# Conditioning vectors summed along rows on VectorE in place of TensorE products

## The chip, the cores and the metric

The kernel runs on one core of a Trainium2 chip. The metric is device time in microseconds (us). The engines of the core work side by side, each on its own queue: TensorE (PE for its matmuls, PEld for its weight loads), VectorE (DVE), ScalarE (ACT), GpSimd (POOL) and SyncE (SP), which here issues the loads from HBM.

## The reference

The program is one layer of a decoder trunk on 256 tokens of 2048 channels, all in fp32. A vector c of 2048 values conditions it: six vectors of 2048 channels (shift, scale and gate of two sub-layers) come from one product with a matrix of 2048 x 12288.

```python
c_act = jax.nn.silu(c)
mod = (c_act @ w_ada[l] + b_ada[l])[:, None, :]
sh1, sc1, g1, sh2, sc2, g2 = jnp.split(mod, 6, axis=-1)
h = layer_norm(x) * (1.0 + sc1) + sh1
y = token_mixer(h, w_in[l], ...)
x = layer_norm(ALPHA * x + g1 * y, ln_g[l, 0], ln_b[l, 0])
h = layer_norm(x) * (1.0 + sc2) + sh2
y = conv_ffn(h, w_up[l], ...)
x = layer_norm(ALPHA * x + g2 * y, ln_g[l, 1], ln_b[l, 1])
```

The token mixer is an input projection (`h @ w_in`), a sparse attention, a matrix memory, merge gates, branch projections and an output projection. `conv_ffn` is a gated MLP with 5632 hidden channels.

## The kernel before

All weights come in tiles of 128 x 1024 fp32 (512 KB) into six buffers `w`, by one queue on SP, in the order of use (`load`, L85). A weight of a projection is split into a high part `wh` (ACT, L96) and a low part `wl` (DVE, L97), with four buffers each, and a product is three fp32r matmuls, high x high, high x low and low x high (`mm_a`, `mm_b`, `mm_c`; all are recorded at L77). The order on each engine is set when the program is built: the code gives an order, and a scheduler moves instructions by its own model of time. On the chip each engine takes its list strictly in order.

**Conditioning.** `w_ada` (192 tiles) passes through the same six buffers. A tile holds 128 input channels (on partitions) by 1024 output channels. For one unit of 1024 outputs, DVE takes 16 tiles in turn and adds tile times c into `acc` (128 x 1024): the first with a `tensor_scalar` (L155), the other 15 with a `scalar_tensor_tensor` whose scalar is a column of c (L157), each reading the `acc` that the last one wrote. Then TensorE sums `acc` over the partitions by a product with ones. For shift and scale (`ada_cols`) the first unit does this with 16 small matmuls that put channels on partitions (tile `ps_ada`); the other seven units make a row (`ps_ada`, 32 x 512), ACT copies it out (L181) and two small DMAs issued by ACT turn it into columns `raw`. For the gates (`ada_rows`, four units) the product is 128 x 512 (`ps_adar`), so that the row stands on every partition, and DVE adds the bias, which is loaded broadcast (`badar`).

**Order of the work.** x (2 MB) is loaded, its mean and variance are taken (L249), it is normalised (L279) and turned channel-first by TensorE (`ps_nT`, `nT`). The input projection goes in four groups of four row chunks (512 channels). A group needs the shift and scale of its own 512 channels (one unit of 16 tiles): ACT scales the chunk (`hm`, L299), writes the high part of `hT` (L301) and DVE the low part (L302). Then come 288 matmuls `ps_b` and 144 matmuls `ps_a`, and the partial sums go to `accC`, `KT`, `accQ`, `accM` and `projA` (ACT in the first group, DVE adds L501 and L532 later). While a group runs, a ticker (`Ticker`, `tk`) hands out the 16 tiles of the next group's unit, one for each weight tile. Units of the second shift and scale, and of the gate g1, go out in the same way from the fourth group to the output projection (`ps_o`), and g2 goes out in the first half of the MLP's up projection (`ps_up`). Between `ps_o` and `ps_up` the residual is normalised twice (L890, L895, L922, L947, L949), with the normalised tile `n2` written in an order of channels that fits the columns of shift and scale: channel 512 q + 4 p + i on partition p. The weights' rows are packed in that order on the host.

Of the kernel before, what the change touches and what calls it, by code (L numbers as in the profile page):

```python
# [14 lines left out]
P = 128  # L15
# [17 lines left out]
GR = (1.0, 1.0)  # L33
# [5 lines left out]
FIRST = 14  # L39
F0 = 1  # L40
PTV = 2
YA, YB = 1, 2
# [9 lines left out]
def build(ctx: ExitStack, tc: tile.TileContext, d, out, dbg=None):  # L52
# [15 lines left out]
    nc.sync.dma_start(cst, d["cst"])  # L68
    ident = cst[:, C_ID:C_ID + P]
# [75 lines left out]
    # ---------------------------------------------------------------- conditioning  # L145
# [4 lines left out]
    def ada_partial(u):  # L150
        acc = p0.tile([P, 1024], F32, name="acc", tag="acc")
        for k in range(KD):
            t = load(d["w_ada"][u * KD + k])
            if k == 0:
                nc.vector.tensor_scalar(acc, t, cs[:, 0:1], None, op0=ALU.mult)  # L155
            else:
                nc.vector.scalar_tensor_tensor(acc, t, cs[:, k:k + 1], acc, op0=ALU.mult, op1=ALU.add)  # L157
            if k < KD - 1:
                yield
        yield acc  # L160

    def ada_cols(u, m_sh, m_sc, q):
        """Shift and 1 + scale of the channels 512 q + 4 p + i, on partition p, in column 4 q + i."""
        for acc in ada_partial(u):
            if acc is None:
                yield
        for _ in range(YA):
            yield
        ps = bank(psa, "ps_ada")
        if q == 0 and m_sh == 0:  # L170
            src = [ps[:, 4 * i:4 * i + 4] for i in range(2)]
            for i in range(2):
                v = acc[:, i * 512:(i + 1) * 512].rearrange("k (c b) -> k b c", b=4)
                for b in range(4):
                    mm(src[i][:, b:b + 1], v[:, b, :], ones[:, 0:1], True, True)
        else:
            raw = p0.tile([P, 2, 4], F32, name="raw", tag="raw", bufs=2)
            for i in range(2):
                mm(ps[32 * i:32 * i + 32, :], ones[:, 0:32], acc[:, i * 512:(i + 1) * 512], True, True)
            row = t2([64, 512], "row")  # L180
            nc.scalar.copy(row, ps[0:64, :])  # L181
            for i in range(2):
                nc.scalar.dma_start(raw[:, i, :], row[32 * i:32 * i + 1, :])
            src = [raw[:, i, :] for i in range(2)]
            for _ in range(YB):
                yield
        for i, m in ((0, m_sh), (1, m_sc)):
            c0 = m * KD + 4 * q
            nc.vector.tensor_add(modc[:, m, 4 * q:4 * q + 4], src[i],
                                 prm[:, R_BADA + c0:R_BADA + c0 + 4])  # L190
        nc.vector.tensor_scalar(modc[:, m_sc, 4 * q:4 * q + 4], modc[:, m_sc, 4 * q:4 * q + 4],
                                1.0, None, op0=ALU.add)
        yield

    def ada_rows(u, dst, col, c):
        """1024 gate values on every partition."""
        for acc in ada_partial(u):
            if acc is None:
                yield
        for i in range(2):  # L200
            c0 = c * 1024 + i * 512
            bt = t2([P, 512], "badar")
            nc.sync.dma_start(bt, d["b_ada"][0:1, col + c0:col + c0 + 512].to_broadcast([P, 512]))
            ps = bank(psa, "ps_adar")
            mm(ps, ones, acc[:, i * 512:(i + 1) * 512], True, True)
            nc.vector.tensor_add(dst[:, c0:c0 + 512], ps, bt)
# [30 lines left out]
    # ---------------------------------------------------------------- input norm  # L237
# [4 lines left out]
    xt = p0.tile([P, 2, D], F32, name="xt", tag="t16")  # L242
    for t in range(2):
        for c in (0, 1024):
            nc.sync.dma_start(xt[:, t, c:c + 1024], d["x"][t * P:(t + 1) * P, c:c + 1024])
# [22 lines left out]
    first = ada_cols(0, 0, 1, 0)  # L268
    for _ in range(FIRST):
        next(first)  # L270
# [10 lines left out]
    def turn(p):  # L281
        ps = bank(psa, "ps_nT")
        for i in range(2):
            for t in range(2):
                q, b = divmod(2 * p + i, 4)
                v = xt[:, t, q * 512:(q + 1) * 512].rearrange("s (c b) -> s b c", b=4)
                nc.tensor.transpose(ps[:, (2 * i + t) * P:(2 * i + t + 1) * P], v[:, b, :], ident)
# [5 lines left out]
    run_all(first)  # L293

    def modulate(dst, src_of, m_sh, m_sc, p):
        tmp = t2([P, 2, S], "hm")
        for i in range(2):
            k = 2 * p + i
            nc.scalar.activation(tmp[:, i, :], src_of(i), AF.Identity, bias=modc[:, m_sh, k:k + 1],  # L299
                                 scale=modc[:, m_sc, k:k + 1])  # L300
        nc.scalar.copy(dst[:, 2 * p:2 * p + 2, 0, :], tmp)  # L301
        nc.vector.tensor_sub(dst[:, 2 * p:2 * p + 2, 1, :], tmp, dst[:, 2 * p:2 * p + 2, 0, :])  # L302

    # ---------------------------------------------------------------- input projection
# [81 lines left out]
    tb = 0  # L386
    def modulate_in(p):
        modulate(hT, lambda i: nT[:, 2 * p + i, :], 0, 1, p)

    def ada_mod(q):  # L390
        yield from ada_cols(q, 0, 1, q)
        for p in (2 * q, 2 * q + 1):
            modulate_in(p)
            yield

    for p in range(2):
        modulate_in(p)
# [4 lines left out]
    # ---------------------------------------------------------------- gates  # L402
# [66 lines left out]
    for gi in range(4):  # L469
        nxt = gi < 3  # L470
        if nxt:
            tk.add(ada_mod(gi + 1))
        comp = []

        def work():
# [3 lines left out]
            tk.tick(GR[0] if nxt else GR[1])  # L479

        kn = 4
        k0 = 4 * gi
        for b0 in range(0, NBLK, 2):
            wh, wl = load_split(d["w_in_b"][tb])
            tb += 1
            work()
            for bb in range(2):
                b = b0 + bb
                if b % 2 == 0:
                    ps = bank(psm, "ps_b")  # L490
                for k in range(kn):
                    mm_b(ps[:, (b % 2) * S:(b % 2 + 1) * S], wh, wl, bb * kn + k, hT, k0 + k,
                         k == 0, k == kn - 1)
                if b % 2 == 1:
                    dst, kind = dest_b(b // 2)
                    src = (ps.rearrange("p (w t k) -> p w t k", w=2, t=2) if kind
                           else ps.rearrange("p (a b) -> p a b", a=2))
                    if gi == 0:
                        nc.scalar.copy(dst, src)
                    else:  # L500
                        nc.vector.tensor_add(dst, src, dst)  # L501
                    if not nxt and b == 3:
                        comp.append(compress())
                        for q in range(4):
                            tk.add(ada_cols(6 + q, 3, 4, q))
                    if not nxt and b == NBLK - 1:
                        conv()
        for c in range(6):
            pss = [bank(psm, "ps_a%d" % t) for t in range(2)]
            aw = AW if c < 4 else 512  # L510
            for pi in range(2):
                if c < 4:
                    wh, wl = load_split(d["w_in_a"][gi * 8 + c * 2 + pi])
                else:
                    wh, wl = load_split(d["w_in_v"][gi * 4 + (c - 4) * 2 + pi])
                work()
                for i in range(2):
                    k = k0 + 2 * pi + i
                    for t in range(2):
                        mm_a(pss[t][:, :aw], hT, k, t, wh[:, i * aw:(i + 1) * aw],  # L520
                             wl[:, i * aw:(i + 1) * aw], k == k0, k == k0 + kn - 1)
                if not nxt and c > 2:
# [10 lines left out]
            if not nxt:  # L533
                if c == 2:
# [4 lines left out]
                    next(steps)  # L539
        if nxt:  # L540
# [665 lines left out]
```

## Time and profile before

| | us |
|---|---|
| median of 3 runs (lowest, highest) | 1520.63 (1519.89, 1527.04) |
| span of the profiled execution | 1516.5 |
| median less span (start and end around the span) | 4.1 |
| TensorE matmuls busy | 1457.4 (96%) |
| VectorE busy | 1112.6 (73%) |
| ScalarE busy | 727.0 (48%) |
| moved by DMA | 376.98 MB, 249 GB/s in the mean |

The profile is of one execution. Its span runs from the first to the last instruction; its own device time was not recorded apart, so the median stands for it. A busy TensorE is not TensorE at its peak, since matmuls overlap: the chain of work that ended last shows the rate at which they follow each other.

### The profile page before, as it was taken

Reading aid. Unit: us, or ns where it says so; the run is one execution under the profiler, and the core shown is the slowest. Engines: PE = TensorE matmul, PEld = TensorE weight load, DVE = VectorE, ACT = ScalarE, POOL = GpSimd, SP = SyncE. Lnnn points to the kernel's source line nnn. Section 1 sums busy time; section 2 is a strip of 40 time slices with the busy share of each in tenths; the row PEclk is TensorE's granted clock in tenths of the full one; section 3 lists DMA queues with packets and bytes.
Section 4 is the critical chain, followed back from the end, with each engine's and each line's share of the span. In section 5 each row is a group of like instructions: output and inputs, shape, how many; then the busy total and the mean of one; then the engine's idle time right before and its main releaser. Section 6 shows DMA issues by size and latency. Waiting matters only on the chain.

```text
span 1516.5 us, 23668 instructions
## 1 busy us (share of the span) xinstructions
PE 1457.4 (96%) x9174; PEld 1299.5 (86%) x9174; DVE 1112.6 (73%) x1478; ACT 727.0 (48%) x1031; POOL 2.1 (0%) x6
## 2 busy tenths in 40 slices
PE   1999999999999999999699999999999999999997
PEld 1999898888889999988688888888898888888887
DVE  7869896897868778868877888865556666665557
ACT  3663443556565443434465455553335555554341
POOL 0000000000000000000000000000000000000000
PEclk9999999999999999999899999999999999999999
DMA  9989888894858899998358888866666666666662
GB/s 365 324 284 333 290 316 274 304 339 134 313 160 309 284 324 330 330 355 298 138 184 279 281 287 275 275 186 192 195 192 195 187 188 185 188 184 191 192 196 87
DMA packets 106961, 376.98 MB, mean 249 GB/s; under 512 B 13792, under 2 KB 13920, under 8 KB 106080
## 3 DMA queue, kind: packets, MB, share of 16 engines
q1 hardware_dynamic: 104832, 375.43, 73.9%
q8 instruction: 72, 1.18, 0.3%
q10 hardware_dynamic: 2016, 0.03, 0.1%
q14 instruction: 41, 0.34, 0.1%
HBM read 373.29 MB, written 2.10 MB: 248 GB/s over the span
## 4 chain that ended last, share of the span: by engine, by line
PE 89%; DVE 6%; DMA 2%; issue 1%; ACT 1%; DVEq 0%; SPq 0%; ACTq 0%
PE ps_up L77 33%; PE ps_d L77 16%; PE ps_mg L77 12%; PE ps_b L77 7%; PE ps_br L77 6%; PE ps_o L77 5%; PE ps_a L77 5%; DMA w<-in_w_ada_dram 2%; DVE acc L157 2%; DVE wl L97 1%; PE ps_y L77 1%; PE ps_s L77 1%; PE ps_ada L77 1%; PE ps_hid L77 1%; DVE xz L890 1%
## 5 line engine op out<-in xcount | busy, mean ns | idle before, releaser
L96 ACT CAST wh<-w 128x1024 fp32r<-128x1024 f32 (+1 forms) x478 | 495.9, 1038 | 571.4 <-PE ps_d L77 124.0
L97 DVE TENSOR_TENSOR wl<-w,wh 128x1024 fp32r<-128x1024 f32 (+1 forms) x478 | 575.4, 1205 | 255.1 <-ACT wh L96 254.7
L77 PE MATMUL ps_up<-h2T,wh 128*128 128x512 f32 x1408 | 496.5, 398 | 0.0
L77 PE MATMUL ps_up<-h2T,wl 128*128 128x256 f32 x1408 | 393.7, 280 | 0.0
L77 PEld LDWEIGHTS ps_up<-h2T,wh 128*128 128x128 f32 x1408 | 265.1, 188 | 64.3 <-ACT wh L96 0.5
L157 DVE SCALAR_TENSOR_TENSOR acc<-w,cs,acc 128x1024 f32<-128x1024 f32 x180 | 230.7, 1282 | 56.5 <-DMA w<-in_w_ada_dram 55.0
L77 PEld LDWEIGHTS ps_up<-h2T,wl 128*128 128x128 f32 x1408 | 266.0, 189 | 0.6 <-issue 0.5
L77 PE MATMUL ps_d<-wh,uTt 128*128 128x512 f32 (+1 forms) x792 | 210.4, 354 | 0.0
L77 PE MATMUL ps_mg<-hT,wh 128*128 128x256 f32 x1024 | 192.4, 287 | 0.0
L77 PEld LDWEIGHTS ps_mg<-hT,wh 128*128 128x128 f32 x1024 | 161.8, 193 | 5.7 <-issue 4.9
L77 PEld LDWEIGHTS ps_d<-wh,uTt 128*128 128x128 f32 x792 | 140.4, 189 | 20.8
L77 PE MATMUL ps_mg<-hT,wl 128*128 128x256 f32 x512 | 146.1, 285 | 0.0
L77 PE MATMUL ps_b<-hT,wh 128*128 128x256 f32 x768 | 140.4, 284 | 1.4 <-ACT hT L301 0.7
L77 PE MATMUL ps_d<-wl,uTt 128*128 128x512 f32 (+1 forms) x396 | 140.0, 354 | 0.0
L77 PEld LDWEIGHTS ps_b<-hT,wh 128*128 128x128 f32 x768 | 119.9, 192 | 5.9 <-issue 3.9
L77 PE MATMUL ps_b<-hT,wl 128*128 128x256 f32 x384 | 108.6, 283 | 0.6 <-DVE wl L97 0.6
L77 PE MATMUL ps_a<-wh,hT 128*128 128x392 f32 (+1 forms) x384 | 109.1, 359 | 0.0
L77 PEld LDWEIGHTS ps_mg<-hT,wl 128*128 128x128 f32 x512 | 98.6, 193 | 0.8 <-issue 0.7
L77 PEld LDWEIGHTS ps_d<-wl,uTt 128*128 128x128 f32 x396 | 74.9, 189 | 10.3
L77 PEld LDWEIGHTS ps_a<-wh,hT 128*128 128x128 f32 x384 | 71.0, 188 | 10.0 <-issue 2.7
L77 PEld LDWEIGHTS ps_b<-hT,wl 128*128 128x128 f32 x384 | 73.6, 192 | 1.2 <-DVE wl L97 0.8
L77 PE MATMUL ps_a<-wl,hT 128*128 128x392 f32 (+1 forms) x192 | 68.6, 358 | 0.0
(248 smaller groups left out, 1400.6 us busy)
## 6 DMA issues: line engine op xcount, KB each, us to landing
w<-in_w_ada_dram SPq DMA_DIRECT2D x192, 512.0 KB, 4.9
w<-in_w_up_dram SPq DMA_DIRECT2D x176, 512.0 KB, 4.2
w<-in_w_down_dram SPq DMA_DIRECT2D x90, 512.0 KB, 3.9
w<-in_w_mg_dram SPq DMA_DIRECT2D x64, 512.0 KB, 5.0
w<-in_w_in_b_dram SPq DMA_DIRECT2D x48, 512.0 KB, 5.0
w<-in_w_br_dram SPq DMA_DIRECT2D x32, 512.0 KB, 5.4
w<-in_w_o_dram SPq DMA_DIRECT2D x32, 512.0 KB, 5.5
w<-in_w_in_a_dram SPq DMA_DIRECT2D x32, 392.0 KB, 4.3
```

The source lines that it names most:

```text
L77: nc.tensor.matmul(o, lhsT, rhs, start=start, stop=stop)
L96: nc.scalar.copy(wh[:, :n], t[:, :n])
L97: nc.vector.tensor_sub(wl[:, :n], t[:, :n], wh[:, :n])
L157: nc.vector.scalar_tensor_tensor(acc, t, cs[:, k:k + 1], acc, op0=ALU.mult, op1=ALU.add)
L890: nc.vector.scalar_tensor_tensor(z, z, mv[:, 0:1], lg[:, c * 512:(c + 1) * 512], op0=ALU.subtract, op1=ALU.mult)
```

## The change

The matrix `w_ada` is packed the other way: a tile now holds 128 output channels (on partitions) by 1024 of the 2048 input channels. c is written on every partition once (`crow`, by 16 transposes and four copies), and for every tile DVE multiplies it with half of `crow` and sums along the row with the instruction's accumulator output, into `parts`. Two small additions make a column of shift, scale or gate. TensorE makes no products for this; the gates are turned into rows on every partition by transposes of their columns (eight for 1024 values), and ACT copies them out. The bias comes from `prm` in all cases.

The groups stay at four chunks, but shift and scale come two chunks at a time (8 tiles), each followed by its `modulate_in`. The ticker hands out 2/3 of a tile for each weight tile. Channels stand in their plain order, so `n2` is written without a stride and `nT` is read without one. The loads of x stand earlier in the code. A buffer of GpSimd's DMA descriptors, which no DMA here uses, is made smaller. The diff, cut:

```diff
+    xt = p0.tile([P, 2, D], F32, name="xt", tag="t16")
+    for t in range(2):
+        for c in (0, 1024):
+            nc.sync.dma_start(xt[:, t, c:c + 1024], d["x"][t * P:(t + 1) * P, c:c + 1024])
...
+    crow = p0.tile([P, D], F32, name="crow")
+    for i in range(4):
+        ps = bank(psm, "ps_c")
+        for j in range(4):
+            nc.tensor.transpose(ps[:, j * P:(j + 1) * P], cs[:, 4 * i + j:4 * i + j + 1].to_broadcast([P, P]),
+                                ident)
+        nc.scalar.copy(crow[:, i * 512:(i + 1) * 512], ps)
+    def ada_chunk(m, k):
+        for i in range(2):
+            t = load(d["w_ada"][(m * KD + k) * 2 + i])
+            nc.vector.scalar_tensor_tensor(t, t, 1.0, crow[:, i * 1024:(i + 1) * 1024], op0=ALU.mult,
+                                           op1=ALU.mult, accum_out=parts[:, m, k, i:i + 1])
+            yield
+    def ada_cols(m, n, k0, k1):
+        for k in range(k0, k1):
+            for i in range(n):
+                yield from ada_chunk(m + i, k)
+        o, v = modc[:, m:m + n, k0:k1], parts[:, m:m + n, k0:k1, :]
+        nc.vector.tensor_add(o, v[:, :, :, 0], v[:, :, :, 1])
+        nc.vector.tensor_add(o, o, bada[:, m:m + n, k0:k1])
+    def ada_rows(m, dst, c):
+        yield from ada_cols(m, 1, 8 * c, 8 * c + 8)
...
+            for j in range(4):
+                nc.tensor.transpose(ps[:, j * P:(j + 1) * P],
+                                    modc[:, m, k + j:k + j + 1].to_broadcast([P, P]), ident)
+            nc.scalar.copy(dst[:, k * P:(k + 4) * P], ps)
...
+    def ada_mod(k0, k1):
+        while k0 < k1:
+            k = min(k0 + 2, k1)
+            yield from ada_cols(0, 2, k0, k)
+            modulate_in(k0, k)
+            k0 = k
...
-            tk.add(ada_mod(gi + 1))
+            tk.add(ada_mod(k0 + kn, k0 + kn + GROUPS[gi + 1]))
+            rate = 4 * GROUPS[gi + 1] / (6 * kn)
...
-        z = xz[:, t, c * 512:(c + 1) * 512].rearrange("s (c b) -> s c b", b=4)
-        o = n2[:, t, c * 512:(c + 1) * 512].rearrange("s (b c) -> s c b", b=4)
+        z, o = xz[:, t, c * 512:(c + 1) * 512], n2[:, t, c * 512:(c + 1) * 512]
```

**The loads at the start.** SP's queue before, from its first load: `prm`, `cst`, x, then 16 tiles of `w_ada` ahead of the first weight tile of the input projection.

```order
L67 DMA prm<-in_prm_dram 128x400
L68 DMA cst<-in_cst_dram 128x608
L245 DMA xt<-in_x_dram 128x1024 x4
L88 DMA w<-in_w_ada_dram 128x1024 x6
L407 DMA gb<-in_ml_gate_b_dram 128x8
L88 DMA w<-in_w_ada_dram 128x1024 x10
L88 DMA w<-in_w_in_b_dram 128x1024
L88 DMA w<-in_w_ada_dram 128x1024
```

And the same place now:

```order
L67 DMA prm<-in_prm_dram 128x400
L68 DMA cst<-in_cst_dram 128x608
L72 DMA xt<-in_x_dram 128x1024 x4
L92 DMA w<-in_w_ada_dram 128x1024 x6
L384 DMA gb<-in_ml_gate_b_dram 128x8
L92 DMA w<-in_w_ada_dram 128x1024 x10
L92 DMA w<-in_w_in_b_dram 128x1024 x2
L92 DMA w<-in_w_ada_dram 128x1024
```

The loads of x stood ahead of `w_ada` in the queue before already, and the same 16 tiles stand ahead of the first weight tile. What moved is behind them: two weight tiles now pass for one or two tiles of `w_ada`.

**VectorE at the start.** Its list now, from the fourth accumulating multiplication (L170) to the first low parts of the projection's weights; L180 and L181 are the two additions that end a column, L281 is the low part of `hT`.

```order
L170 SCALAR_TENSOR_TENSOR w,parts<-w,crow 128x1024 x5
L180 TENSOR_TENSOR modc<-parts 128x2x2
L170 SCALAR_TENSOR_TENSOR w,parts<-w,crow 128x1024
L181 TENSOR_TENSOR modc<-modc,prm 128x2x2
L170 SCALAR_TENSOR_TENSOR w,parts<-w,crow 128x1024 x2
L281 TENSOR_TENSOR hT<-hm,hT 128x2x256
L170 SCALAR_TENSOR_TENSOR w,parts<-w,crow 128x1024 x5
L180 TENSOR_TENSOR modc<-parts 128x2x2
L181 TENSOR_TENSOR modc<-modc,prm 128x2x2
L101 TENSOR_TENSOR wl<-w,wh 128x1024
L170 SCALAR_TENSOR_TENSOR w,parts<-w,crow 128x1024
L101 TENSOR_TENSOR wl<-w,wh 128x1024
```

Before, 15 `scalar_tensor_tensor` on `acc` stood there in one piece, then one `wl`, and then the two bias additions that waited for `ps_ada`. Now the first two chunks are done after 8 tiles, the other two after 16, and the second low part of `hT` follows behind the last two rows shown.

**TensorE at the start.** Its list now, with the buffer numbers of the tiles, from the first matmul of the input projection to the 17th; 16 transposes `ps_c` and the 32 transposes `ps_nT` stand ahead of these rows.

```order
L81 MATMUL ps_b_282<-hT_112,wh_285 128x256 x2
L81 MATMUL ps_b_282<-hT_112,wl_286 128x256
L81 MATMUL ps_b_282<-hT_112,wh_285 128x256 x2
L81 MATMUL ps_b_282<-hT_112,wl_286 128x256
L81 MATMUL ps_b_314<-hT_112,wh_317 128x256 x2
L81 MATMUL ps_b_282<-hT_112,wh_285 128x256
L81 MATMUL ps_b_314<-hT_112,wl_318 128x256
L81 MATMUL ps_b_314<-hT_112,wh_317 128x256 x2
L81 MATMUL ps_b_314<-hT_112,wl_318 128x256
L81 MATMUL ps_b_314<-hT_112,wh_317 128x256
L81 MATMUL ps_b_349<-hT_112,wh_352 128x256 x2
L81 MATMUL ps_b_282<-hT_112,wh_285 128x256
```

Before, 8 of the 32 transposes `ps_nT` stood first, then the matmuls `ps_ada`, then the other 24, then `ps_b`. Now no product with ones stands ahead of `ps_b`, and 16 matmuls stand ahead of the first that needs the low part of the third chunk's `hT` (the last row): those of the first two chunks for two blocks, two of a third block, and one of each block with the third chunk's high part.

## Rows read from the trace of the kernel before

**Rows 1.** The page: the span, busy time of the engines, and the chain of work that ended last by engine.

```profile
span 1516.5 us, 23668 instructions
PE 1457.4 (96%) x9174; PEld 1299.5 (86%) x9174; DVE 1112.6 (73%) x1478; ACT 727.0 (48%) x1031; POOL 2.1 (0%) x6
PE 89%; DVE 6%; DMA 2%; issue 1%; ACT 1%; DVEq 0%; SPq 0%; ACTq 0%
```

**Rows 2.** Busy time of the engines by stretch: the start, the four groups of the input projection, the attention, the branch projections, and the normalisations between `ps_o` and `ps_up`. Columns: stretch, its length, PE, PEld, DVE, ACT, POOL (busy us and instructions), granted TensorE clock, share of the DMA engines, GB/s.

```profile
0.00:44.30 44.30, 10.76 (x48) 9.59 (x48) 32.83 (x49) 16.68 (x26) 1.16 (x5) 1.00 0.94 356
44.30:109.20 64.90, 64.13 (x437) 60.94 (x438) 46.61 (x46) 40.04 (x59) 0.00 (x0) 1.00 0.90 313
109.20:172.90 63.70, 63.70 (x438) 60.58 (x436) 56.54 (x66) 27.64 (x33) 0.00 (x0) 1.00 0.86 301
172.90:237.50 64.60, 64.03 (x437) 60.87 (x437) 59.34 (x70) 27.15 (x31) 0.00 (x0) 1.00 0.89 308
315.20:466.00 150.80, 150.67 (x1028) 129.42 (x1027) 117.89 (x191) 85.76 (x181) 0.00 (x0) 0.98 0.69 240
466.00:655.00 189.00, 189.00 (x1550) 186.07 (x1549) 152.12 (x163) 82.41 (x92) 0.00 (x0) 1.00 0.90 314
744.10:773.00 28.90, 15.79 (x78) 12.86 (x77) 22.28 (x63) 18.94 (x35) 0.00 (x0) 0.70 0.00 1
```

**Rows 3.** The start in order of time, from the timeline: start us, duration us, engine, line, operation, tiles, count, and in brackets the idle time before it and what ended it.

```profile
13.53 0.75 DVE L155 TENSOR_SCALAR acc<-w,cs 128x1024 f32<-128x1024 f32 x1
17.73 17.13 DVE L157 SCALAR_TENSOR_TENSOR acc<-w,cs,acc 128x1024 f32<-128x1024 f32 x13
18.71 1.55 PE L287 MATMUL ps_nT<-cst,xt 128*128 128x128 f32 x6 [2.46 <-ACT xt L279]
33.78 1.05 ACT L96 CAST wh<-w 128x1024 fp32r<-128x1024 f32 x1 [12.05 <-DMA w<-in_w_in_b_dram]
34.91 3.90 PE L77 MATMUL ps_ada<-cst,acc 128*128 128x1 f32 x16 [14.64 <-DVE acc L157]
40.27 2.08 ACT L299 ACTIVATE hm<-nT,modc 128x256 f32<-128x256 f32 x4
43.67 0.63 ACT L301 CAST hT<-hm 128x512 fp32r<-128x512 f32 x1
44.35 0.62 PE L77 MATMUL ps_b<-hT,wh 128*128 128x256 f32 x3 [0.72 <-ACT hT L301]
45.69 0.38 PE L77 MATMUL ps_b<-hT,wh 128*128 128x256 f32 x1 [0.72 <-DVE hT L302]
```

**Rows 4.** Stretches by the same columns as Rows 2, of TensorE alone: the load phase, TensorE's work ahead of the projection, and the normalisations.

```profile
14.00:34.00 20.00, 2.26 (x8) 1.00 1.03 408
34.90:41.90 7.00, 6.99 (x32) 1.00 0.89 328
748.00:765.00 17.00, 7.51 (x28) 0.51 0.00 0
```

**Rows 5.** VectorE in the third group, timeline as in Rows 3.

```profile
184.88 1.22 DVE L97 TENSOR_TENSOR wl<-w,wh 128x1024 fp32r<-128x1024 f32 x1
186.01 0.69 DVE L501 TENSOR_TENSOR KT<-ps_b,KT 128x512 f32<-128x512 f32 x1
186.62 1.28 DVE L157 SCALAR_TENSOR_TENSOR acc<-w,cs,acc 128x1024 f32<-128x1024 f32 x1
187.81 1.23 DVE L97 TENSOR_TENSOR wl<-w,wh 128x1024 fp32r<-128x1024 f32 x1
```

**Rows 6.** Groups of instructions by line: line, engine, operation, tiles, shapes, count, then busy us and mean ns of one, then idle time before them.

```profile
L157 DVE SCALAR_TENSOR_TENSOR acc<-w,cs,acc 128x1024 f32<-128x1024 f32 x180 | 230.7, 1282 | 56.5 <-DMA w<-in_w_ada_dram 55.0
L890 DVE SCALAR_TENSOR_TENSOR xz<-xz,mv_z,lnr 128x512 f32<-128x512 f32 x8 | 5.9, 741 | 0.0
L895 DVE SCALAR_TENSOR_TENSOR xz<-xz,mv_z,lnr 128x512 f32<-128x512 f32 x8 | 5.6, 742 | 0.0
L895 DVE DVE_READ_ACCUMULATOR xz<-xz,mv_z,lnr 128x1 f32 x8 | 0.7, 82 | 0.0
L189 DVE TENSOR_TENSOR modc<-raw,prm 128x4 f32<-128x4 f32 x14 | 2.2, 160 | 10.8 <-DMA raw<-row 10.7
L922 ACT ACTIVATE sqj<-xz,sq 128x512 f32<-128x512 f32 x8 | 5.6, 707 | 6.2 <-DVE sq L920 6.2
L947 ACT ACTIVATE n<-xz,mv_n 128x512 f32<-128x512 f32 x4 | 5.1, 1272 | 0.0
```

**Rows 7.** Pieces of the chain that ended last, in order of time: start us, us, engine and tile, count. One of the seven later `ps_ada` with the work beside it, one of the four `ps_adar`, behind 24 products of 256 columns, and one group of eight transposes.

```profile
85.85 2.84 PE ps_a L77 x16
88.70 0.98 PE ps_ada L77 x4
...
565.01 2.88 PE ps_mg L77 x24
567.89 1.72 PE ps_adar L77 x4
...
428.05 0.87 PE ps_yT L753 x8
```

**Rows 8.** The same view between `ps_o` and `ps_up`.

```profile
754.43 0.90 ACT sqj L922 x3
755.35 0.17 DVE sq L934
...
755.94 1.26 ACT n L947
757.24 1.13 PE ps_n L959 x4
...
759.61 1.20 ACT n L947
760.85 0.47 PE ps_n L959
761.32 2.56 PE ps_up L77 x8
...
772.81 2.22 PE ps_up L77 x13
```

More of the change, by code (lines that the diff above doesn't have):

```diff
@@ L148, in build @@
     modc = p0.tile([P, 6, KD], F32, name="modc")
[L150 to L166, printed above, removed]
+    parts = p0.tile([P, 6, KD, 2], F32, name="parts")
+    bada = prm[:, R_BADA:R_BADA + 6 * KD].rearrange("p (m k) -> p m k", m=6)
+    for m in (1, 4):
+        nc.vector.tensor_scalar(bada[:, m, :], bada[:, m, :], 1.0, None, op0=ALU.add)
+    crow = p0.tile([P, D], F32, name="crow")
[5 more added lines that the diff above has]
+        nc.scalar.copy(crow[:, i * 512:(i + 1) * 512], ps)
@@ L167, in ada_cols @@
+    def ada_rows(m, dst, c):
+        yield from ada_cols(m, 1, 8 * c, 8 * c + 8)
         for _ in range(YA):
             yield
[L169 to L186, printed above, removed]
@@ L266, in ln_aggr @@
         return mv
-    first = ada_cols(0, 0, 1, 0)
-    for _ in range(FIRST):
-        next(first)
     mvx = []
@@ L292, in build, with modulate_in @@
         turn(p)
[L293 to L302, printed above, removed]
+    def modulate_in(k0, k1):
+        tmp = t2([P, 2, S], "hm")[:, :k1 - k0, :]
+        for k in range(k0, k1):
+            nc.scalar.activation(tmp[:, k - k0, :], nT[:, k, :], AF.Identity,
+                                 bias=modc[:, 0, k:k + 1], scale=modc[:, 1, k:k + 1])
+        nc.scalar.copy(hT[:, k0:k1, 0, :], tmp)
+        nc.vector.tensor_sub(hT[:, k0:k1, 1, :], tmp, hT[:, k0:k1, 0, :])
+    def ada_mod(k0, k1):
[4 more added lines that the diff above has]
+            k0 = k
+    run_all(ada_mod(0, GROUPS[0]))
     gates0 = pg.tile([P, NG0, 512], F32, name="gates0", tag="gates0")
@@ L467, in gate_steps, with stream @@
         yield
-    for gi in range(4):
-        nxt = gi < 3
+    def stream(src, width, per):
+        tiles = iter(range(src.shape[0]))
+        while True:
+            wh, wl = load_split(src[next(tiles)][:, :width * per])
+            work()
+            for i in range(per):
+                yield wh[:, i * width:(i + 1) * width], wl[:, i * width:(i + 1) * width]
+    wb, wa, wv = (stream(d[n], w, p) for n, w, p in (("w_in_b", P, 8), ("w_in_a", AW, 2), ("w_in_v", 512, 2)))
+    k0 = 0
+    for gi, kn in enumerate(GROUPS):
+        nxt = gi < len(GROUPS) - 1
         if nxt:
-            tk.add(ada_mod(gi + 1))
+            tk.add(ada_mod(k0 + kn, k0 + kn + GROUPS[gi + 1]))
+            rate = 4 * GROUPS[gi + 1] / (6 * kn)
+        else:
+            rate = GR1
         comp = []
@@ L478, in work @@
             comp.clear()
[L479 to L507, printed above, removed]
+            tk.tick(rate)
+        for b in range(NBLK):
+            if b % 2 == 0:
+                ps = bank(psm, "ps_b")
+            for k in range(k0, k0 + kn):
+                wh, wl = next(wb)
+                mm_b(ps[:, (b % 2) * S:(b % 2 + 1) * S], wh, wl, 0, hT, k, k == k0, k == k0 + kn - 1)
+            if b % 2 == 1:
+                dst, kind = dest_b(b // 2)
+                src = (ps.rearrange("p (w t k) -> p w t k", w=2, t=2) if kind
+                       else ps.rearrange("p (a b) -> p a b", a=2))
+                if gi == 0:
+                    nc.scalar.copy(dst, src)
+                else:
+                    nc.vector.tensor_add(dst, src, dst)
+                if not nxt and b == 3:
+                    comp.append(compress())
+                    tk.add(ada_cols(3, 2, 0, KD))
+                if not nxt and b == NBLK - 1:
+                    conv()
         for c in range(6):
@@ L510, in build @@
             aw = AW if c < 4 else 512
[L511 to L522, printed above, removed]
+            for k in range(k0, k0 + kn):
+                wh, wl = next(wa if c < 4 else wv)
+                for t in range(2):
+                    mm_a(pss[t][:, :aw], hT, k, t, wh, wl, k == k0, k == k0 + kn - 1)
+                if not nxt and c > 2 and (k - k0) % 2:
                     next(steps, None)
```

90 lines of the change are left out of this document (28 added, 62 removed).

## The prediction

> **What bounds the kernel now.** I read the page's chain of waits first: 89% of the span that ended last is TensorE, 6% VectorE, 2% DMA [rows 1]. The busy share alone would mislead here (VectorE 73%), so I then read the stretches by stage [rows 2]. The reader should see three kinds of stage. From 44.3 us to the output projection TensorE is busy for practically the whole of each stretch (64.13 of 64.9, 63.7 of 63.7, 64.03 of 64.6, 150.67 of 150.8, 189 of 189): whatever TensorE no longer has to do there is time won, as long as nobody else becomes late. VectorE is close behind in the second and third group (56.5 of 63.7 and 59.3 of 64.6 us), far behind in the first (46.6 of 64.9). Only two stretches are not TensorE's: the start, where it works 10.8 of 44.3 us, and the normalisations after 744 us, where it works 15.8 of 28.9.
>
> The start I read in order of time [rows 3]: the conditioning tiles run through VectorE one after the other until 34.9, TensorE sums them over the partitions (3.90 us), ACT scales four chunks (2.08), and the projection runs at full pace from 45.69.
>
> **The change part by part.**
>
> *"x loaded first"*: SP's queue had x ahead of `w_ada` already, and the first weight tile stays behind 16 tiles of `w_ada`. I cost it at zero. DMA is the floor here: it moves 408 GB/s from 14 to 34 us [rows 4], which is 524 KB / 408 = 1.285 us for each tile, and the first weight tile is cast at 33.78 [rows 3]. No reordering of VectorE lets the projection start before that.
>
> *The start.* VectorE's 16 tiles end before at 17.73 + 17.13 = 34.9. Now the first costs 1.28 in place of 0.75 [rows 3, 6]: +0.5. The low part of `hT` for the first two chunks now lies among them: +0.7 (the 0.69 of a 512-wide addition in rows 5). Two small additions at 0.16 [rows 6]: +0.3. In exchange a tile no longer reads what the one before it wrote: the 13 in a row take 17.13 / 13 = 1.32 each, while the same instruction beside others takes 187.81 - 186.62 = 1.19 [rows 5]. DMA allows 1.285, so that only the delay of about 1.2 us is caught up. Last tile done at 34.9 + 0.5 + 0.7 + 0.3 - 1.2 = 35.2. Then two additions (35.5), two activations `hm` at 0.52 each (36.5, half of 2.08), a cast `wh` that stands ahead on ACT (1.05: 37.6), the high part of `hT` (0.63: 38.2). The low part waits on VectorE behind two `wl` and one more tile: 35.5 + 1.13 + 1.19 + 1.13 = 39.0, then 0.69: 39.7. By then 16 products are done (first-half chunks, which are ready long before), against 4 at 45.69 before; at 2.88 / 24 = 0.12 for a product of 256 columns [rows 7], 12 x 0.12 = 1.4 us. Gain: 45.7 - 39.7 + 1.4 = 7.4.
>
> Against this stands TensorE's clock. Before, it had worked without a break since 34.9 when the projection began; now it stands idle from about 26 us (last `nT`) to 34.9. [...] Term: 7.4 - 1.9 = **5.5**, from 3.9 to 7.4, and lower to 2 if a cast or a copy on ACT stands in the way of `hT`.
>
> `crow`: 16 transposes at 0.26 (4.2 us) and four copies at 0.6 from about 4 us on end near 9, before the first tile's 13.5, beside the loads of x. Cost nothing; if ACT's square root came late by it, 1 us.
>
> *TensorE's products with ones.* Seven later `ps_ada` at 0.98 on the chain, four `ps_adar` at 1.72 [rows 7]. In place of the latter come eight transposes, for which the nearest row is eight `ps_yT`: 0.87. All lie where TensorE is the bound. 7 x 0.98 = **6.9** and 4 x (1.72 - 0.87) = **3.4**. Bounds: 3.4 could be 2.4 if the transposes go like `ps_n` (four in 1.13 at the lower clock [rows 8]); 6.9 could be 5 if VectorE paces the second and third group.
>
> *VectorE's price.* 12 tiles at 0.75 become 1.28; the accumulator output adds a read of 82 ns each. At 512 columns the instruction takes 742 ns with it and 741 without (L895, L890) [rows 6]; so a tile should take 1.28 + 0 to 0.08. In the second group VectorE goes from 56.5 to at most 56.5 + 0.5 + 1.3 = 58.3 of 62.7, in the third from 59.3 to 61.1 of 63.6 us. That is still under TensorE's, but with 2.5 us of room; its queue also waits for `ps_b` and for tiles of `w_ada`, with only four `wl` ahead. I charge **-1**, from 0 to -4. The ticker's 2/3 spreads the tiles over all 24 weights of a group, which puts them into the 392-wide part too. There a weight tile costs VectorE 0.87 (784/1024 of the 1.13 from one `wl` to the next instruction), 0.8 (2/3 of 1.19) and some 0.5 for the addition of a result, 2.2 in all [rows 5], against TensorE's 12 x 2.84 / 16 = 2.13 [rows 7]; before, the last tiles of that part had no conditioning tile beside them.
>
> *The normalisation.* The four `n2` on ACT (L947) take 1272 ns, while ACT's other pass over 512 columns of the same tile takes 707 [rows 6]; the difference is the scattered write, which goes. Two of them stand in the chain, and a third ahead of the three `sqj` [rows 8]: 3 x 0.56 = 1.7. I take **+1.6**, from 0 (if VectorE's statistics end later than ACT) to 2.3 (four of them).
>
> *Gone beside the path*: `raw` and `badar` DMAs, L181 (seven copies of 0.58, replaced by eight of the same size): zero, as TensorE does not wait for them before.
>
> Sum: 5.5 + 6.9 + 3.4 + 1.6 - 1 = 16.4. The span of 1516.5 becomes 1500.1, and with the 4.1 us around it, by which the median stands above the span, 1504.2. I predict **1504**.
>
> [...] The two rows of 512 columns say that the accumulator output costs the multiplication nothing. [...]
>
> **The rivals.**
>
> 1. *The start gives little.* The lower clock lasts, or the second half of `hT` waits behind casts: the term is 0 to 2 instead of 5.5, and the time 1508 to 1510. For it: ACT has `wh` between the two. Against it: TensorE has 16 products to do meanwhile.
>
> 2. *VectorE takes the bound in the second and third group.* Then the 2 us of `ps_ada` there are not won and another 2 to 4 are lost: 1508 to 1511; together with a weak start 1513 to 1515. For it: 92% busy in the third group before. Against it: TensorE was idle for 0.6 us of both groups together [rows 2].
>
> 3. *The accumulating multiplication is slow, and the kernel slower.* It decides from the point where each tile costs x more: the second and third group lose 16x less their room (62.7 - 57.0 and 63.6 - 59.9), the start 16x less 1.4, together 48x - 10.8. The 17.4 us that the other terms win are gone at x = 0.59 us. [...]
>
> 4. *More is won*: the start keeps 7.4, the normalisation 2.3, and VectorE loses nothing: 1500. [...]
>
> **How the numbers follow.** Forecast (1499 to 1509): 0.60. First rival 0.15, second 0.13, third 0.04, more won 0.08. A change of 0.5% is 7.6 us, about what a measurement of this kernel can tell from none: faster means under 1513. The forecast, the fourth and nearly all of the first rival lie there, and most of the second: 0.60 + 0.08 + 0.14 + 0.05 = 0.87, which I take as 0.86; the same 0.10, slower 0.04. The sum of the low bounds is 2 + 5 + 2.4 + 0 - 4 = 5.4 (1515), of the high ones 7.4 + 6.9 + 3.4 + 2.3 = 20 (1500); the schedule of the attention is new in places, and I give it some us to both sides. Range 1495 to 1514.
>
> **What would show it.** Right: the first `ps_b` near 35, full pace near 40, the first `ps_a` about 5.5 us earlier; groups two and three of 62.7 to 63.6 us with no `ps_ada`; L170 at 1.28 us; the four ACT passes of `n2` near 0.7; the stretch from the last `ps_o` to steady `ps_up` shorter by 1.6. Wrong: a low clock in the first group beyond 44 us; TensorE waiting for `wl` in groups two and three; L170 over 1.4 us.

## The result, and the profile after

The kernel after takes 1542.65 us (median of 4, 1541.71 to 1543.81) against 1521.82 of the kernel before in the same comparison: a ratio of 1.0137, 95% interval 1.0118 to 1.0156. The prediction of 1504, from 1495 to 1514, was wrong in size and in sign: the change made the kernel slower. The profiled execution has a span of 1539.8 us, 23.3 more than before.

The page's chain of waits and two of its groups, of the kernel after (they answer to [rows 1] and to L157 of [rows 6]; the columns are the same):

```profile
span 1539.8 us, 23697 instructions
PE 1457.4 (95%) x9162; PEld 1301.3 (85%) x9162; DVE 1102.7 (72%) x1666; ACT 725.8 (47%) x1036; POOL 2.1 (0%) x6
PE 65%; DMA 18%; DVE 11%; issue 4%; ACT 1%; DVEq 0%; SPq 0%; ACTq 0%
...
L101 DVE TENSOR_TENSOR wl<-w,wh 128x1024 fp32r<-128x1024 f32 (+1 forms) x478 | 574.4, 1205 | 223.2 <-ACT wh L100 222.7
L170 DVE SCALAR_TENSOR_TENSOR w<-w,crow 128x1024 f32<-128x1024 f32 x192 | 234.1, 1223 | 166.1 <-DMA w<-in_w_ada_dram 165.0
```

TensorE and VectorE are busy as long as before, to 10 us. What changed is what the end waits for: 18% of the chain are now transfers, against 2%, and VectorE stands idle 165.0 us until a tile of `w_ada` arrives, against 55.0. The multiplication itself takes 1223 ns, less than the 1282 of the old one. Nor did loads become slower: from issue to landing a tile of `w_ada` takes 4.8 us (median), before 4.9.

Stretch by stretch, from the first and last products of each kind (the last column is experiment 2 below, in which VectorE's order is held from the attention on):

| stretch, us | before | after | after, order held |
|---|---|---|---|
| until the first `ps_b` | 44.3 | 34.9 | 36.4 |
| four groups of the input projection | 64.8, 63.7, 64.6, 78.0 | 67.2, 65.5, 63.1, 77.8 | 66.9, 64.6, 63.4, 77.9 |
| end of the input projection | 315.5 | 308.6 | 309.2 |
| attention, merge, output projection | 428.9 | 453.3 | 425.0 |
| last `ps_o` to first `ps_up` | 16.6 | 15.5 | 15.5 |
| first up projection | 252.6 | 263.0 | 253.0 |
| from there to the end | 502.9 | 499.4 | 499.4 |

So 6.9 us were won by the end of the input projection, 1.1 at the normalisations and 3.5 at the end; 24.4 were lost in the middle and 10.4 in the first up projection. The first row is the whole middle of before; then come the stretches of after that answer to [rows 2, 4], and below them the whole middle and the first up projection of after:

```profile
315.50:744.40 428.90, 428.75 (x3057) 392.07 (x3055) 339.33 (x449) 206.31 (x313) 0.00 (x0) 0.99 0.81 284
...
34.90:43.40 8.50, 7.24 (x30) 6.65 (x31) 7.79 (x9) 4.53 (x6) 0.00 (x0) 0.50 1.02 396
102.20:167.70 65.50, 62.97 (x434) 59.81 (x433) 57.06 (x83) 27.05 (x32) 0.00 (x0) 1.00 0.88 302
167.70:230.80 63.10, 62.71 (x434) 59.87 (x433) 59.06 (x86) 26.57 (x30) 0.00 (x0) 1.00 0.91 316
...
308.60:761.90 453.30, 429.47 (x3049) 393.26 (x3047) 332.86 (x525) 202.80 (x313) 0.00 (x0) 0.98 0.78 266
...
777.40:1040.40 263.00, 256.01 (x1445) 221.72 (x1445) 195.39 (x299) 138.80 (x213) 0.00 (x0) 0.99 0.74 244
```

In the middle TensorE is busy 429.5 us, as before (428.75 of 428.9 there), and idle 23.8 that it was not; VectorE is busy 332.9 of 453.3, so the sum of its work isn't the bound. Both wait. TensorE's longest waits in the middle of after (who waited for whom: us in total, times, longest):

```profile
PE ps_mg L81 <- DVE wl L101: 8.4, 10, 1.7
PE ps_br L81 <- DVE y_nsaT L674: 5.1, 1, 5.1
PE ps_pT L661 <- DVE pt L638: 2.5, 2, 1.5
PE ps_o L81 <- DVE wl L101: 2.5, 2, 1.8
```

And its products with `wl` in the up projections, from the page (columns as in [rows 6]); all the idle time ahead of them ends with VectorE:

```profile
L81 PE MATMUL ps_up<-h2T,wl 128*128 128x256 f32 x1408 | 396.9, 282 | 7.0 <-DVE wl L101 7.0
```

Before, TensorE had no such wait in the middle. In after 21.3 us of its waits there end with VectorE and 2.4 with ACT. What VectorE itself waits for, its timeline shows in the first up projection (start, duration, engine, line, operation, tiles, shapes, count, and in brackets the idle time before it):

```profile
993.18 0.08 DVE L170 DVE_READ_ACCUMULATOR w<-w,crow 128x1 f32 x1
...
995.32 1.22 DVE L101 TENSOR_TENSOR wl<-w,wh 128x1024 fp32r<-128x1024 f32 x1
999.05 1.23 DVE L170 SCALAR_TENSOR_TENSOR w<-w,crow 128x1024 f32<-128x1024 f32 x1 [2.51 <-DMA w<-in_w_ada_dram]
1000.20 0.08 DVE L170 DVE_READ_ACCUMULATOR w<-w,crow 128x1 f32 x1
1000.20 0.48 DVE L1014 SCALAR_TENSOR_TENSOR av<-ag,prm,av 128x255 f32<-128x255 f32 x1
1000.60 1.22 DVE L101 TENSOR_TENSOR wl<-w,wh 128x1024 fp32r<-128x1024 f32 x1
```

and the chain of waits in the same place, in pieces (start, duration, what):

```profile
988.38 3.63 DMA w<-in_w_ada_dram
...
993.29 5.73 DMA w<-in_w_ada_dram
...
1000.31 3.96 DMA w<-in_w_ada_dram
```

Read together: VectorE stands 2.51 us at a conditioning tile; right behind it, without a gap, go a step on `av` and a `wl` that TensorE needs. The load for which it stands began at 993.29, when the conditioning tile before had been read (993.18 + 0.08), and took 5.73 us. All tiles, of weights and of `w_ada`, share six buffers `w`; a load can be issued only when an older tile has been used up. Here a conditioning tile stands in VectorE's queue ahead of the `wl` of older weight tiles. These hold the five other buffers, the load is issued late, and VectorE waits for what is left of it with the older work behind it. That VectorE keeps to the order of its queue here shows in the same 2.51 us: the `wl` of 1000.60 reads a `wh` that ACT had finished at 996.65 (995.62 + 1.03), and the oldest of the four buffers `wl` had been free since 993.54, when TensorE's last product with it ended; yet VectorE, idle until 999.05, began this `wl` only behind the multiplication.

This can be counted. From the order of loads on SP and of reads on VectorE I took, for each conditioning multiplication behind the first 16, how many older tiles VectorE still had to read at that point, and set beside it the idle time ahead of that instruction that ended with a load (mean us, count in brackets):

| older tiles unread | before, 6 buffers | after, 6 buffers | after, 8 buffers (experiment) |
|---|---|---|---|
| 0 or 1 | 0.07 (105) | 0.04 (28) | 0.03 (30) |
| 2 | 0.39 (35) | 0.57 (43) | 0 (15) |
| 3 | 1.02 (35) | 1.09 (78) | 0.02 (20) |
| 4 | 0.22 (1) | 1.80 (24) | 0.37 (22) |
| 5 | none | 3.66 (3) | 1.04 (64) |
| 6 | | | 2.30 (21) |
| 7 | | | 2.39 (4) |

In these three runs the wait goes with the number of buffers left over, whichever the kernel. Before, 36 of 176 multiplications stood ahead of three or more older tiles; after, 105. The number isn't the whole of it: with the shorter multiplication of experiment 4 three unread tiles cost 1.5 us in the mean, and in the last run of experiment 7 one or two already cost 0.7.

TensorE's waits cost more than their own length. The middle of after is 28.3 us longer than with the order held (425.0): 19.7 of it are idle time, and 8.6 come because the same matmuls keep TensorE busy longer (429.5 against 420.9). Its granted clock is 0.50 from 422.3 to 425.7 us, behind an idle time of 2.0; from 470.1 to 476.9, within and behind one of 5.1; and from 688.5 to 691.9, behind one of 1.8. In all it stands at 0.50 for 20.5 us of this middle, for 10.2 with the order held. How much of the 8.6 us is the clock's, no run separates.

### The profile page after: what moved, and what is told of

Same layout as the page of the kernel before. It is cut to its first block, busy times and chain, and to the rows that moved or that the text cites. A ratio compares the mean times of both kernels' runs of the same rounds, so it can differ in the third digit from the quotient of the medians.

```text
span 1539.8 us, 23697 instructions
## 1 busy us (share of the span) xinstructions
PE 1457.4 (95%) x9162; PEld 1301.3 (85%) x9162; DVE 1102.7 (72%) x1666; ACT 725.8 (47%) x1036; POOL 2.1 (0%) x6
## 4 chain that ended last, share of the span: by engine, by line
PE 65%; DMA 18%; DVE 11%; issue 4%; ACT 1%; DVEq 0%; SPq 0%; ACTq 0%
PE ps_up L81 29%; DMA w<-in_w_ada_dram 17%; PE ps_d L81 15%; PE ps_b L81 7%; DVE wl L101 4%; PE ps_o L81 4%; PE ps_a L81 4%; DVE w L170 3%; PE ps_br L81 2%; PE ps_mg L81 2%; DVE xz L867 1%; DVE xz L872 1%; PE ps_hid L81 1%; DMA xt<-in_x_dram 1%; PE ps_w L81 0%
## 5 line engine op out<-in xcount | busy, mean ns | idle before, releaser
L170 DVE SCALAR_TENSOR_TENSOR w<-w,crow 128x1024 f32<-128x1024 f32 x192 | 234.1, 1223 | 166.1 <-DMA w<-in_w_ada_dram 165.0
L81 PE MATMUL ps_mg<-hT,wh 128*128 128x256 f32 x1024 | 187.9, 283 | 0.0
L81 PEld LDWEIGHTS ps_mg<-hT,wl 128*128 128x128 f32 x512 | 97.3, 190 | 12.3 <-DVE wl L101 10.5
L81 PEld LDWEIGHTS ps_d<-wl,uTt 128*128 128x128 f32 x396 | 74.9, 189 | 10.3
```

Of the source, the lines that this page charges most:

```text
L81: nc.tensor.matmul(o, lhsT, rhs, start=start, stop=stop)
L170: nc.vector.scalar_tensor_tensor(t, t, 1.0, crow[:, i * 1024:(i + 1) * 1024], op0=ALU.mult, op1=ALU.mult, accum_out=parts[:, m, k, i:i + 1])
```

## The experiments

Four theories. **O**: VectorE's order, as above. **V**: VectorE's work, the multiplication with accumulator above all. **T**: the loads themselves, by their new layout. **D**: the tiles lie more densely, since the pauses after every 16 of them are gone.

**1. The order held.** After the multiplication of `ada_chunk` one call was added, which keeps it behind the VectorE instruction written before it and costs no instruction:

```diff
-            nc.vector.scalar_tensor_tensor(t, t, 1.0, crow[:, i * 1024:(i + 1) * 1024], op0=ALU.mult,
-                                           op1=ALU.mult, accum_out=parts[:, m, k, i:i + 1])
+            ins = nc.vector.scalar_tensor_tensor(t, t, 1.0, crow[:, i * 1024:(i + 1) * 1024], op0=ALU.mult,
+                                                 op1=ALU.mult, accum_out=parts[:, m, k, i:i + 1])
+            tc.keep_in_program_order(ins)
```

> The kernel after, with each conditioning multiplication (L170) pinned in VectorE's queue behind the VectorE instruction written before it, so that it no longer stands ahead of the low parts `wl` of older weight tiles. Theory O (VectorE's order costs the loads their lead: it stands at a conditioning tile whose load could only be issued when older tiles were used up): the 24.4 us lost between 308 and 762 us and the 11 us of the first up projection come back nearly whole, 1500 to 1512 us, and VectorE's idle time before L170 that ends with a load of `w_ada` falls from 165 us to under 70. Rival V (VectorE's own work, the multiplication with accumulator, is too much): the same work in another order, 1538 to 1547. Rival T (the loads themselves, new layout or more of them at a time): 1538 to 1547.

Measured 1514.98 us (1510.25 to 1516.09), ratio to before 0.9946 (0.9926 to 0.9967), 3 us over the range of O and far from V and T. The tiles are loaded in the same order as in the kernel after, one for one, so T falls. VectorE's two largest groups:

```profile
L101 DVE TENSOR_TENSOR wl<-w,wh 128x1024 fp32r<-128x1024 f32 (+1 forms) x478 | 575.9, 1205 | 318.1 <-ACT wh L100 314.8 <-PE ps_mg L81 0.9
L170 DVE SCALAR_TENSOR_TENSOR w<-w,crow 128x1024 f32<-128x1024 f32 x192 | 232.3, 1217 | 2.9 <-DMA w<-in_w_ada_dram 2.9
```

The same instructions, as long, and the 165.0 us are 2.9; VectorE's idle time now ends with ACT, as most of it did in the kernel before (254.7 us ahead of its `wl`). The held multiplications aren't all that moved: the scheduler also placed instructions of ACT and TensorE elsewhere, so that this run alone doesn't show VectorE's order as the only cause; experiment 3 comes closer. The middle takes 426.6 us and the first up projection 252.6. The fourth group, with the compression and the convolution in it, became 85.8 instead of 77.8: there holding the order does harm, and the cause of that stays open.

**2. The order held from the attention on.** The same call, made only after the input projection.

> The kernel after with the conditioning multiplications pinned in VectorE's queue only from the attention on; in the input projection, where the first pinned kernel lost 8 us in the fourth group (85.8 us against 77.4), they stand as in the kernel after. Theory O: the two parts add, the start and the groups of the kernel after (fourth group's end near 308) and the rest of the pinned one (1513.1 - 318.8 = 1194.3 from there on): span 1500 to 1506, 1502 to 1508 us. Rivals V and T, after the first runs without support: over 1530.

Measured 1505.62 us (1504.02 to 1509.08), ratio 0.9896 (0.9874 to 0.9917), as O expected (1502 to 1508). It is the fastest version of this study, and within 2 us of the time that was predicted for the change. Its group of multiplications:

```profile
L172 DVE SCALAR_TENSOR_TENSOR w<-w,crow 128x1024 f32<-128x1024 f32 x192 | 233.2, 1219 | 24.4 <-DMA w<-in_w_ada_dram 22.8 <-PE ps_hid L81 0.6 <-DVE wl L101 0.5
```

and its middle as a stretch (columns as in [rows 2]):

```profile
309.20:734.20 425.00, 420.90 (x3048) 389.69 (x3046) 333.48 (x525) 205.38 (x313) 0.00 (x0) 0.99 0.81 284
```

Nearly all that is left of the waits lies in the input projection. TensorE's idle time in the middle is 4.1 us instead of 23.8, with VectorE as busy as in the kernel after (333.5 against 332.9). The tiles are loaded in the order of the kernel after, one for one; of TensorE's list of 9162 matmuls 474 places differ, all but two of them in the middle.

**3. Only from the up projection on.**

> The kernel after with the pins only from the first up projection on. Theory O: the stages lose and recover each for itself; the up projection takes the 253.0 us that it took with all pins (263.0 in the kernel after), the attention and the merge stay at 453 us: 1530 to 1535 us. If what is lost in the middle is the cause of the loss in the up projection too, 1539 to 1545.

Measured 1532.99 us (1529.58 to 1541.62), ratio 1.0090 (1.0065 to 1.0116), as O expected: the stages lose each for itself. The up projection took 253.8 us, and VectorE's 48.4 us of waits for `w_ada` in it are gone. Here SP's loads and all 9162 matmuls of TensorE stand in the order of the kernel after; only VectorE's and ACT's lists differ, and only in that stage. So there the order on these two is shown to cost the 9 us; for the middle, where TensorE's list changed too, it is in part argued. The profiled execution is the 1541.62 one; its middle (461.9) isn't compared, since TensorE was granted 0.92 in the attention against 0.97.

**4. Half of the multiplication taken away.** It runs over 512 of 1024 columns, which leaves out half of each sum.

```diff
-            nc.vector.scalar_tensor_tensor(t, t, 1.0, crow[:, i * 1024:(i + 1) * 1024], op0=ALU.mult,
+            nc.vector.scalar_tensor_tensor(t[:, :512], t[:, :512], 1.0, crow[:, i * 1024:i * 1024 + 512], op0=ALU.mult,
```

> The kernel after, with each conditioning multiplication over the first 512 of its 1024 columns (half of each sum is left out); the loads stay whole. It takes 192 x 0.5 = some 96 us of work from VectorE. Theory O: the waits for loads stay where they are, since the tiles come when they came: 1528 to 1543 us. Rival V: VectorE is no longer the bound, 1498 to 1510. Rival T: 1538 to 1543.

Measured 1532.67 us (1530.72 to 1536.0), ratio 1.0071 (1.0045 to 1.0098). 102 us less work for VectorE gave 10 us, none of them in the up projection (263.9). The group:

```profile
L170 DVE SCALAR_TENSOR_TENSOR w<-w,crow 128x512 f32<-128x512 f32 x192 | 132.3, 689 | 215.5 <-DMA w<-in_w_ada_dram 215.0
```

Where the multiplication got shorter, the wait for the load got longer. V (1498 to 1510) falls; the time lies in the range of O.

**5. Eight buffers.**

```diff
-WB = (6, 4, 4)
+WB = (8, 4, 4)
```

> The kernel after with eight buffers `w` in place of six. Theory O: a load can be issued two tiles earlier, some half of the 165 us of waits and of the 35 us go, 1512 to 1532 (it may be less, since VectorE's queue now passes over up to ten older tiles instead of seven or eight). Rivals V and T: 1538 to 1546.

Measured 1533.77 us (1532.5 to 1539.21), ratio 1.0088 (1.0053 to 1.0122): a gain of 9, less than O had put, and 2 us outside its range. The waits fell to 134.0 us only, the up projection stayed at 264.3. The table above fits this: with two more buffers the scheduler puts the conditioning tiles about two places further ahead.

**6. Buffers of their own for `w_ada`**: two `wa` beside six `w`.

> The kernel after with two buffers `wa` for the tiles of `w_ada` alone beside the six `w` (the memory of the run with eight `w`, and the scheduler free to order VectorE). Theory O: VectorE still takes the conditioning tiles ahead of older `wl`, but their loads no longer wait for a buffer that an older weight tile holds, so that the waits for `w_ada` fall from 165 us to under 50 and the time to 1503 to 1515 us. If it is early order as such that costs, not the buffers: 1530 to 1543 as with eight `w`. Rival T: 1530 to 1543.

Measured 1545.14 us (1543.09 to 1549.53), ratio 1.0159 (1.0134 to 1.0185): as a time, a miss for O. VectorE's waits for `w_ada` fell to 83.3 us, where O had put under 50. The stages tell two things apart: with two buffers the start, which needs only `w_ada`, ends at 44.2 and the first group takes 84.1 us; from 332.8 on the middle takes 441.3 and the up projection 254.1. But the loads stand in another order here: 108 conditioning tiles lay in the middle (88 in after) and none in the up projection, so that this run doesn't separate early order from missing buffers.

**7. What had held the order before.** In the kernel before, first the chain alone was cut (each product goes into its own tile, but still reads `acc`, which holds the first tile of the 16; the sum over the 16 tiles is left out):

```diff
-                nc.vector.scalar_tensor_tensor(acc, t, cs[:, k:k + 1], acc, op0=ALU.mult, op1=ALU.add)
+                nc.vector.scalar_tensor_tensor(t, t, cs[:, k:k + 1], acc, op0=ALU.mult, op1=ALU.add)
```

> The kernel before, with the chain of the conditioning sums cut: each multiplication writes its product plus the first tile's into its own tile instead of into `acc` (this leaves out the sum over the 16 row chunks). Work and loads stay. Theory O in its strong form (the chain through `acc` is what held VectorE's order): waits for `w_ada` as in the kernel after, 1535 to 1550 us. Theory O in a weak form (the chain is one cause among several; the queue written for this kernel shows tiles of `w_ada` a little earlier than before, not as early as after): 1522 to 1532. Rivals V and T: no change, 1519 to 1524.

Measured 1518.36 us (1516.0 to 1527.56), ratio 0.9993 (0.9972 to 1.0015). No change in sum, so the strong form falls; by stages 8.1 us won by the end of the input projection (where TensorE needn't wait for the sum of the first 16 tiles) and 8.0 lost in the middle (436.9). Then `acc` was not read at all (the last operand became `t`):

> The kernel before with the multiplications reading only their own tile and `cs`, not `acc` at all (the sum over the 16 row chunks is left out); the run that cut the chain but left each multiplication a read of the unit's first tile in `acc` cost nothing (0.9993). In the queue written for this kernel the tiles of `w_ada` stand as far ahead in the stage of the merge gates as in the kernel after, and nearly as before in the up projection. Theory O with the common tile `acc` as what held the order: the waits come in the middle, 10 to 20 us lost there, against some 8 gained at the start as in the cut kernel: 1522 to 1538 us. If `acc` has nothing to do with it: 1514 to 1520, as with the cut chain.

Measured 1536.37 us (1526.28 to 1538.54), ratio 1.0088 (1.0061 to 1.0114). The middle takes 452.8 us, about as in the kernel after, with none of its other edits, and VectorE's waits for `w_ada` in it are 86.3 us (17.8 before, 94.7 after). TensorE's loss there has another make-up: 13.6 us idle, and 439.2 busy against 428.75 before, with a granted clock of 0.95 in the attention against 0.98. The profiled execution took 1538.54 us, of six from 1526.28 to 1538.54. The waits in the whole kernel:

```profile
L157 DVE SCALAR_TENSOR_TENSOR w<-w,cs 128x1024 f32<-128x1024 f32 x180 | 229.9, 1281 | 124.2 <-DMA w<-in_w_ada_dram 123.7
```

The one tile `acc`, of which there is one buffer, had kept the conditioning tiles from running ahead in the middle. It accounts for the waits there; of the up projection's 10.4 us it shows 2.9 (255.5). What moved the tiles further ahead there stays open; that holding the order brings it back, to 1 us, is shown by experiments 1 to 3.

**8. Less dense tiles**: five empty steps behind every 16 tiles of the second shift and scale.

> The kernel after with five empty steps behind every 16 conditioning tiles of the second shift and scale, as the kernel before had them for its products and DMAs (YA, YB and a last step), so that the tiles lie less densely and the tiles of the gates follow. Rival D (the loss comes from the denser tiles): the middle recovers, 1522 to 1534 us. Theory O: little, the order stays early, 1536 to 1544 us.

Measured 1534.91 us (1532.71 to 1540.6), ratio 1.0092 (1.0064 to 1.0120), between the ranges of D and O. The middle takes 443.5, so density is worth 10 of the 24 us while the order is early; the up projection stays at 262.3. D is a part, not the cause: with the order held, the same dense tiles cost nothing (425.0).

**9. Is the held order a gain by itself?** In the kernel before, from the attention on:

> The kernel before with its multiplications into `acc` (L157) pinned in the same way from the attention on. It stood at its loads of `w_ada` 56.5 us in all, in waits of mostly under 1.1 us. Theory O: these waits were covered by TensorE's work (0.6 us of idleness in two groups, the up projection at 2.8 us a tile throughout), so that no more than 0 to 4 us is to be won, 1516 to 1522 us. If pinning helps by itself, whatever the changed kernel did, 1506 to 1514 us.

Measured 1521.6 us (1518.74 to 1528.15), ratio 1.0000 (0.9979 to 1.0020). No: its waits for `w_ada` ahead of these multiplications fell from 55.0 to 10.5 us and the time stayed, so they had been covered there.

**10. Order held and eight buffers.**

> The kernel with the pins from the attention on, and eight buffers `w` in place of six. With the order pinned Theory O sees no more use for buffers behind the input projection; in the input projection, which isn't pinned, the run with eight buffers ended its fourth group 3.7 us earlier than the kernel after (304.5 against 308.2). So 1498 to 1504 us, 4 us under the pinned one. If eight buffers help everywhere, 1494 or less; if nothing, 1504 to 1508.

Measured 1510.01 us (1508.95 to 1510.38), ratio 0.9930 (0.9918 to 0.9942), slower than with six and outside every range that was put. The input projection did end 4 us earlier (305.1), but the middle takes 435.3. TensorE's waits there (who waited for whom: us in total, times, longest), from 435 to 651:

```profile
PE ps_pT L666 <- DVE pt L643: 5.3, 1, 5.3
PE ps_y L81 <- ACT pT L596: 3.4, 2, 3.2
```

These are waits inside the attention; with six buffers only the second is there. The traces show that the weight products which could have covered them had been done earlier: at the fifth group of eight `ps_pT` 688 of the 768 products of the merge gates that stand in the attention were through, with six buffers 532, and at the wait of 5.3 us all 768. Of the 10.3 us, 5.6 are idle time; for the other 4.7 TensorE is busy longer (425.6 against 420.9), at a granted clock of 0.98 against 0.99 in the middle.

## Why the prediction was wrong

**The step that failed** is *VectorE's price*, "I charge -1, from 0 to -4". It was worked out from busy time, in the second and third group: room of 2.5 us, a queue that "also waits for `ps_b` and for tiles of `w_ada`". What a wait costs depended on where the multiplication stands in VectorE's queue among older tiles, and for the attention that was left as "some us to both sides" for the schedule; for the up projection nothing was charged. It measured 24.4 + 10.4 us in the middle and the up projection, and 2.8 us in the second group (65.5 for 62.7), the place of the second rival, while the third kept its forecast (63.1 for 63.6). The start's paragraph counted as a gain that "a tile no longer reads what the one before it wrote"; the same freedom let the scheduler move the tiles ahead of older weights elsewhere: experiment 7 shows this for the middle; in the up projection what moved them stays open.

**Right**: the start. First `ps_b` at 34.94, a granted clock of 0.50 from there until 43.4, the first `ps_a` at 73.8 after 80.0: 6.2 us for 5.5 (5.0 in experiment 2, whose queues are the same up to there). The 1.9 us that this term takes off for the clock no run shows by itself: the runs showed the 0.50 until 43.4 and the 6.2 us. The normalisations: from VectorE's last six steps on `xz` to steady `ps_up` the chain of after takes 788.60 - 760.08 = 28.5 us, before 30.3 (742.47 to the 772.81 of [rows 8]): 1.8 for 1.6. The table's row ends at the first `ps_up` and has 1.1 of it. These are the two ends in the chain of after:

```profile
760.08 2.02 DVE xz L872 x6
...
788.60 134.02 PE ps_up L81 x759
```

The four `n2` passes on ACT (1272 ns in [rows 6]) now take 804, a little more than the 0.7 us I had put:

```profile
L923 ACT ACTIVATE n<-xz,mv_n 128x512 f32<-128x512 f32 x4 | 3.2, 804 | 0.0
```

**Products with ones**, 6.9 + 3.4: with the order held the middle is 3.9 us shorter (four `ps_ada` and two gate vectors were to bring 5.6), the up projection 0.4 longer where 1.7 were to go. Of these 7.3 us 3.5 came.

**Not foreseen**: 3.5 us won behind the first up projection (below).

With the order held from the attention on, the span is 1502.1 for 1500.1 predicted, and the time 1505.6 us for 1504. That agreement has luck in it. By stages 16.4 us were forecast, 7.4 to the end of the input projection, 5.6 in the middle, 1.6 at the normalisations and 1.7 in the up projection; 6.3, 3.9, 1.1 and -0.4 came, 10.9 in sum, and 3.5 behind them that were not forecast brought it to 14.4.

**The third rival** had the kernel slower, and it came out slower, by another mechanism. The multiplication with accumulator takes 1223 ns, less than the 1282 before, and its read of 82 begins before it ends (in the timeline above at 1000.20, with the multiplication from 999.05 to 1000.28), and experiment 4 shows that its length hardly counts. A result that fits confirms no mechanism.

## What to carry to other kernels

When an edit removes a dependency, ask what the scheduler will do with the freedom: list the order before and after, and for each load count the older tiles of the same buffers that its reader has still to take. With six buffers three unread tiles cost 1.1 us here, five cost 3.7 (three cases), on an engine that was only 72% busy. A long idle time before one group that ends with a DMA of unchanged length (165.0 us in all, at 4.8 us a load after 4.9) was here a question of order and buffers; hold the order first, before adding buffers, and stage by stage: in the fourth group of the input projection it cost 8 us.

## What the runs showed of the hardware

The multiplication of 128 x 1024 takes 1223 ns with a constant and the accumulator output, and 1282, 1279 and 1281 ns in three forms with a scalar column from SBUF and no accumulator (chained, with the chain cut, and with one tile for both tensor operands). So the chain doesn't lengthen the single instruction, but in a row chained ones follow each other more slowly: in the load phase they start 1.32 us apart (17.13 / 13 in [rows 3]), those with the chain cut 1.20 (experiment 7, first kernel), and those with the constant and the accumulator output 1.15 (the kernel after). The forms differ in more than one thing, so that no run separates the accumulator's part from the constant's.

The second up projection, whose code is unchanged, takes 245.8 us in every run with the changed code and 248.9 in every run of the old one, 2.79 against 2.83 us for the 16 products of a weight tile; in the first it is 2.77 before and 2.79 to 2.83 after (median of a tile). TensorE is busy for the whole of it in both (248.60 of 248.60 us and 245.50 of 245.50, between its first and last tile). No run tells why.
